# Two attention units to a turn, and three PSUM users on other banks, in a hybrid decoder layer

## The chip, the cores and the metric

The kernel runs on one core of a Trainium2 chip. The metric is the time of one execution in device microseconds (us), as the median of several runs. One further execution is taken by the hardware profiler; its page and its trace are what is read here. The engines are TensorE (PE in the rows; PEld is its weight load), VectorE (DVE), ScalarE (ACT), GpSimd (POOL) and SyncE (SP), which issues nearly all DMAs.

## What is computed

One decoder layer on x of 1024 x 2048 in float32: an RMS norm, one input projection to 6656 columns, two groups of attention heads side by side, a gated RMS norm of each, one output projection, and a second RMS norm added to x.

```python
def reference(x, w_in, w_out, norm_pre, norm_post, gn_sb, gn_sw, sinks, rel_bias):
    h = x
    for l in range(DEPTH):                                   # DEPTH = 1
        u = rmsnorm(h, norm_pre[l])
        proj = jnp.einsum('bsd,de->bse', u, w_in[l])
        q_sb, k_sb, v_sb, z_sb, q_sw, k_sw, v_sw, z_sw = jnp.split(proj, SPLIT_POINTS, axis=-1)
        o_sb = stick_breaking_attention(q_sb, k_sb, v_sb)    # 16 heads of 64
        o_sw = sliding_window_gqa(q_sw, k_sw, v_sw, sinks[l], rel_bias)  # 16 heads, 4 of K and V, window 128
        o_sb = rmsnorm(o_sb, gn_sb[l]) * jax.nn.silu(z_sb)
        o_sw = rmsnorm(o_sw, gn_sw[l]) * jax.nn.silu(z_sw)
        y = jnp.einsum('bse,ed->bsd', jnp.concatenate([o_sb, o_sw], axis=-1), w_out[l])
        h = h + rmsnorm(y, norm_post[l])
    return h
# stick-breaking: A[t,s] = beta_ts * prod_{s<j<t}(1 - beta_tj), beta = sigmoid(q.k / 8), s < t
# sliding window: softmax over q.k / 8 + bias, with one sink logit a head
```

## The kernel before

**Tiles and stages.** The input projection is done in 52 blocks of 128 columns. Each operand is split into a high and a low part, so a block is 16 x 2 x 3 matmuls of 128x512 (p_qsw, p_ksb and so on in the rows; three "first" blocks are f0a to f2b, done together while x arrives). Queries and keys go to DRAM and come back where attention wants them. The last stage, the output projection (rows y), is not touched.

**Units.** Attention is cut into 224 units: 64 of sliding-window heads (sw, in groups g = 0 to 3 of 16) and 160 of stick-breaking heads (sb, pairs 0 to 7 of 20 units; in a pair two heads, in a head four groups of 256 rows with 4, 3, 2 and 1 units). A unit has three stages on TensorE:

- s1: four score matmuls into a "pz" bank (z). Then ScalarE and VectorE make the weights: for sb two sigmoids, two scans and a product (tiles m and b; a unit on the diagonal is also masked on GpSimd), for sw a biased softmax (tile L, with an exponential that waits for the row maximum nm).
- s2: three or four transposes of the weights into a "pw" bank (wt; two in a group's last sw unit); ScalarE and VectorE split them into wh and wl.
- s3: four output matmuls (o; two in a group's last sw unit) into the "po" bank. After a sw unit, and after the last unit of a sb row group, ScalarE copies the bank out (finish_o, line 513, tile ot, two buffers), and the copy goes to DRAM.

**PSUM.** Eight banks: "pp" three (projections), "pz" two, "pw" two (also the transposes vt of V), "po" one.

**What sets the order.** TensorE's matmuls keep the order in which the program writes them. After every three projection matmuls `step()` calls `advance()`, which decides by `pe_time`, a running estimate of TensorE's time, whether attention gets a turn. A unit has a period (PER_SB 4.7, PER_SW 3.8), least distances between its stages (lag 6.2 or 7.0 from s1 to s2, lag2 4.5 or 5.0 from s2 to s3), and a depth: at most 3 units between s1 and s2. Before, a turn finishes all outputs that are due, the transposes of one unit, and starts one unit. At a V block's end `drain()` forces what is left of the group or pair. On the other engines a scheduler sets the order; copies out of PSUM have raised priority there.

Of the kernel before, what the change touches and what calls it, by code (L numbers as in the profile page):

```python
# [57 lines left out]
def layer(ctx, tc, xT, x, w_first, w_blk, w_out, g_pre, g_post, g_sb, g_sw, sinks, rel, onehot, penalty, out):  # L58
# [20 lines left out]
    def ptile(tag, name, bufs, shape=None):  # L79
        return pp.tile(shape or [P, HALF], F32, tag=tag, name=name, bufs=bufs)  # L80

    def pproj(name):
        return ptile("pp", name, 3)

    def pz(name, shape=None):
        return ptile("pz", name, 2, shape)

    def pw(name, shape=None):
        return ptile("pw", name, 2, shape)

    def po(name, shape=None):
        return ptile("po", name, 1, shape)
# [24 lines left out]
    def mm(ps, a, b, start, stop):  # L117
        n = 1
        for d in b.shape[1:]:
            n *= d  # L120
        pe_time[0] += n / 2400.0 * (4 if n < 256 or b.dtype == F32 else 1)
        tc.keep_in_program_order(nc.tensor.matmul(ps, a, b, start=start, stop=stop))  # L122
# [20 lines left out]
    waiting, todo = [], []  # L143
    stage1, stage2 = [], []
    last_start = [-100.0]
# [6 lines left out]
    def advance(force=False):  # L152
        now = pe_time[0]
        while waiting and (force or waiting[0][0] <= now):
            todo.extend(waiting.pop(0)[1])
            prep()
        if later and (force or later[0][0] <= now):
            later.pop(0)[1]()
            return True
        if force or not todo:  # L160
            return finish_stage2(force, now) or finish_stage1(force, now) or (bool(todo) and start(now))
        if len(stage1) - stage1_due(now) < todo[0]["depth"] and last_start[0] + todo[0]["period"] <= now:
            while finish_stage2(False, now):
                pass
            finish_stage1(False, now)
            return start(now)
        return False

    def start(now):
        if len(stage1) >= todo[0]["depth"]:  # L170
            return False
        u = todo.pop(0)
        if not u["ready"]:
            u["prep"]()
        last_start[0] = max(last_start[0] + u["period"], now - u["period"])
        u["s1"]()
        stage1.append((pe_time[0], u))
        prep()
        return True

    def stage1_due(now):
        return 1 if stage1 and len(stage2) < 3 and stage1[0][0] + stage1[0][1]["lag"] <= now else 0

    def finish_stage2(force, now):
        if stage2 and (force or stage2[0][0] + stage2[0][1]["lag2"] <= now):
            u = stage2.pop(0)[1]
            u["s3"]()
            left[u["key"]] -= 1
            return True
        return False  # L190

    def finish_stage1(force, now):
        if stage1 and len(stage2) < 3 and (force or stage1_due(now)):
            u = stage1.pop(0)[1]
            u["s2"]()
            stage2.append((pe_time[0], u))
            return True
        return False

    def prep():  # L200
        for u in todo[:AHEAD]:
            if not u["ready"]:
                u["ready"] = True
                u["prep"]()
# [66 lines left out]
    def step():  # L271
        advance()
        background()

    def drain(key):
        n = left.get(key, 0)
        while left.get(key, 0):
            assert advance(True)
        if n and DBG:
            print("DRAIN", key, n, f"{pe_time[0]:.0f}")  # L280
# [4 lines left out]

    xh, xl, xraw = [], [], []
    acc = stg.tile([P, S], F32, tag="acc", name="acc_x", bufs=1)
    ps0 = [[pproj("f0a"), pproj("f0b")], [pproj("f1a"), pz("f1b")], [pz("f2a"), pw("f2b")]]

    oh = at.tile([32, RW], F32, tag="beta", name="oh", bufs=3)  # L290
    pen = at.tile([P, RW], F32, tag="m", name="pen", bufs=3)
# [44 lines left out]
        nc.vector.tensor_scalar_mul(nsink, nsink, -1.0)  # L336

    def bias_table():
        pr = po("bias_ps")
        rel8 = at.tile([32, 16, 8], F32, tag="wl", name="rel8", bufs=3)  # L340
        nc.vector.tensor_copy(rel8, relt.unsqueeze(2).to_broadcast([32, 16, 8]))
        mm(pr[:, :RW], rel8, oh, start=True, stop=True)
        rt = at.tile([P, RW], F32, tag="m", name="rt", bufs=3)
        nc.vector.tensor_add(rt, pr[:, :RW], pen)
        nc.scalar.dma_start(biasd.rearrange("h (a r) n -> (h a) r n", a=8), rt.unsqueeze(1).to_broadcast([P, 16, RW]))

    def rstd_half(h):
        cols = slice(h * HALF, (h + 1) * HALF)
        ps = (pw, po)[h](f"ssq{h}")
        mm(ps, ones, acc[:, cols], start=True, stop=True)  # L350
        nc.scalar.activation(rstd[:, cols], ps, AF.Sqrt, bias=eps, scale=1.0 / D)
        nc.vector.reciprocal(rstd[:, cols], rstd[:, cols])
# [7 lines left out]
    for k in range(KT):  # L360
        if k + WAHEAD < KT:
            first.append(split_first(k + WAHEAD))
        if k + XAHEAD < KT:
            load_x(k + XAHEAD)
        if k == 5:
            load_small()
        if k == 10:
            bias_table()
        if k == KT - 3:
            rstd_half(0)  # L370
            rstd_half(1)
        wh, wl = first.pop(0)
        parts = [(b, h) for h in range(2) for b in range(len(FIRST))]
        for b, h in sorted(parts) if k == KT - 1 else parts:
            for i, (wt, xt) in enumerate(((wh, xh[k]), (wh, xl[k]), (wl, xh[k]))):
                mm(ps0[b][h], wt[:, b, :], xt[:, h * HALF:(h + 1) * HALF],
                   start=(k == 0 and i == 0), stop=(k == KT - 1 and i == 2))
        for i in (k,) if k < 8 else range(2 * k - 8, 2 * k - 6) if k < 12 else ():
            square_x(i)
# [92 lines left out]
    def proj(b, name, nxt=None, mid=None):  # L472
        def get(b, name, kg):
            return split_w(f"{name}_{kg}", w_blk[b, :, 4 * kg:4 * kg + 4, :])

        if not splits:
            splits.append(get(b, name, 0))
        ps = [pproj(f"p_{name}_{h}") for h in range(2)]
        for kg in range(4):
            wh, wl = splits.pop(0)  # L480
            if kg == 2 and mid is not None:
                mid()
            if kg < 3:
                splits.append(get(b, name, kg + 1))
            elif nxt is not None:
                splits.append(get(*nxt, 0))
            for h in range(2):
                for j in range(4):
                    k = 4 * kg + j
                    for i, (wt, xt) in enumerate(((wh, xh[k]), (wh, xl[k]), (wl, xh[k]))):  # L490
                        mm(ps[h], wt[:, j, :], xt[:, h * HALF:(h + 1) * HALF],
                           start=(k == 0 and i == 0), stop=(k == KT - 1 and i == 2))
                    step()
        return ps
# [349 lines left out]
    for n, (b, name, done) in enumerate(work):  # L844
# [3 lines left out]
        ps = proj(b, name, nxt, mids.get(name))  # L848
# [16 lines left out]
    def bank(name):  # L865
        tg = PT2[next(slots) % 8]
        return ptile(tg, name, PB[tg])
# [64 lines left out]
    for i in range(LAST + 1):  # L932
        nxt, src = [], []
        for dc in range(2):
            k0 = (2 * i + dc) * 8
            if i == LAST and dc == 1:
                split_wo(k0 + 8)
                for tb in range(4):
                    for h in range(1 + (tb == 3)):
                        part = slice(h * 256, (h + 1) * 256) if tb == 3 else whole  # L940
                        ps = bank(f"y{i}_{dc}_{tb}_{h}")[:, :part.stop - part.start]
# [8 lines left out]
            for e in range(8):  # L950
# [24 lines left out]
                if i == LAST and dc == 0:  # L975
                    tb, h = divmod(e, 2)
# [59 lines left out]
```

## Time and profile before

| | |
|---|---|
| median of 3 runs | 1795.58 us (1795.38 to 1796.92) |
| the profiled execution | 1792.82 us |
| its span, first to last instruction | 1791.0 us |
| granted TensorE clock, mean | 0.998 |
| TensorE busy, 112 to 480 us (sw attention) | 365.33 of 368 us |
| TensorE busy, 480 to 1430 us (sb attention) | 947.25 of 950 us |
| VectorE busy in the same two | 245.11, 677.64 us |
| ScalarE busy in the same two | 168.99, 407.95 us |

In a timeline row the first number is the start in us from the span's beginning, the second the duration in us, then engine, line, operation, out<-in, shape and count; in brackets stands how long the engine sat idle before it and what ended that. Matmuls overlap, and their ends are modelled, so what one costs is read from start to start.

### The profile page before, as it was taken

To read this page: it belongs to the slowest core of one execution; us is meant where nothing else is said; L and a number is where in the kernel's file an instruction comes from. 1 tells how busy PE (TensorE), PEld (TensorE's weight loads), DVE (VectorE), ACT (ScalarE), POOL (GpSimd) and SP (SyncE) were. 2 spreads that over 40 slices of the span, in tenths; PEclk is the share of its full clock that TensorE was granted. 3 is DMA by queue.
4 is the path that set the end of the run, shared out by engine and by line. 5 is a ranking of instruction groups with operands and counts; after the bars stand their busy time and mean duration, and the time that the engine had idled before them with its cause. 6 is when DMAs were issued, how large, how long until landed. Compare 5 with 4: busy or idle time off the path is not lost.

```text
span 1791.0 us, 27350 instructions
## 1 busy us (share of the span) xinstructions
PE 1769.0 (99%) x9046; PEld 1498.0 (84%) x9046; DVE 1230.8 (69%) x1984; ACT 783.2 (44%) x1696; POOL 498.5 (28%) x648
## 2 busy tenths in 40 slices
PE   8999999999999999999999999999999999999998
PEld 7788888888888888888888888888888887888886
DVE  7558842678467678586675777767868756845896
ACT  7345531455334444344443444434434434444442
POOL 0012121211213324323232333232313224503633
PEclk9999999999999999999999999999999999999999
DMA  7647675576746666556556564554445386634484
GB/s 232 195 149 217 201 228 159 161 204 195 226 131 190 172 177 183 167 170 203 157 162 191 155 186 131 154 165 141 149 109 139 93 257 204 208 101 141 135 283 157
DMA packets 203884, 312.48 MB, mean 174 GB/s; under 512 B 24640, under 2 KB 84192, under 8 KB 203616
## 3 DMA queue, kind: packets, MB, share of 16 engines
q1 hardware_dynamic: 201680, 307.60, 57.6%
q10 hardware_dynamic: 2064, 3.15, 0.5%
q8 instruction: 72, 1.18, 0.3%
q14 instruction: 68, 0.56, 0.1%
HBM read 219.42 MB, written 91.23 MB: 173 GB/s over the span
## 4 chain that ended last, share of the span: by engine, by line
PE 91%; DVE 4%; DMA 2%; ACT 1%; issue 1%; SPq 0%; DVEq 0%; POOL 0%; ACTq 0%; POOLq 0%
PE y L928 16%; PE p_zsw L122 10%; PE p_zsb L122 10%; PE p_vsb L122 9%; PE p_ksb L122 9%; PE p_qsw L122 8%; PE p_qsb L122 8%; PE o_sb L122 4%; PE z_sb L122 4%; PE wt_sb L126 3%; PE p_vsw L122 1%; PE z_sw L122 1%; PE o_sw L122 1%; PE wt_sw L126 1%; DVE wl_sw L661 1%; PE f0a L122 1%
## 5 line engine op out<-in xcount | busy, mean ns | idle before, releaser
L582 DVE TENSOR_TENSOR wl_sb<-wt_sb,wh_sb 128x512 fp32r<-128x512 f32 (+1 forms) x160 | 100.8, 633 | 96.6 <-ACT wh_sb L581 96.4
L566 DVE TENSOR_TENSOR b_sb<-b_sb,m_sb 128x512 f32<-128x512 f32 x160 | 129.5, 809 | 41.2 <-POOL b_sb L556 17.7
L581 ACT CAST wh_sb<-wt_sb 128x512 fp32r<-128x512 f32 (+1 forms) x160 | 87.0, 544 | 135.5 <-PE wt_sb L126 133.0
L563 DVE TENSOR_TENSOR_SCAN m_sb<-m_sb,m_sb,zero 128x257 f32<-128x257 f32 x192 | 142.4, 780 | 2.4 <-ACT m_sb L550 2.1
L928 PE MATMUL y<-wohi,x 128*128 128x512 f32 x448 | 140.7, 390 | 0.4 <-ACT wohi L792 0.4
L928 PE MATMUL y<-wohl,x 128*128 128x512 f32 x576 | 132.5, 389 | 0.0
L928 PEld LDWEIGHTS y<-wohl,x 128*128 128x128 f32 x576 | 108.1, 188 | 22.4
L560 DVE TENSOR_TENSOR_SCAN m_sb<-m_sb,mask 128x256 f32<-128x256 f32 x128 | 119.1, 967 | 6.4 <-ACT m_sb L550 6.3
L643 ACT ACTIVATE L_sw<-L_sw,nm_sw 128x256 f32<-128x256 f32 (+1 forms) x128 | 62.8, 491 | 94.9 <-DVE nm_sw L638 93.5
L122 PE MATMUL p_vsb<-xh,whi_vsb 128*128 128x512 f32 x256 | 101.9, 398 | 0.0
L122 PE MATMUL p_ksb<-xh,wlo_ksb 128*128 128x512 f32 x256 | 100.7, 393 | 0.0
L122 PE MATMUL p_qsb<-xh,whi_qsb 128*128 128x512 f32 x256 | 100.6, 393 | 0.0
L122 PE MATMUL p_vsb<-xh,wlo_vsb 128*128 128x512 f32 x256 | 100.6, 393 | 0.0
L122 PE MATMUL p_qsb<-xh,wlo_qsb 128*128 128x512 f32 x256 | 100.6, 393 | 0.0
L122 PE MATMUL p_zsw<-xh,wlo_zsw 128*128 128x512 f32 x256 | 100.6, 393 | 0.0
L122 PE MATMUL p_vsb<-xl,whi_vsb 128*128 128x512 f32 x256 | 100.5, 392 | 0.0
L122 PE MATMUL p_ksb<-xl,whi_ksb 128*128 128x512 f32 x256 | 100.4, 392 | 0.0
L122 PE MATMUL p_qsb<-xl,whi_qsb 128*128 128x512 f32 x256 | 100.4, 392 | 0.0
L122 PE MATMUL p_zsw<-xl,whi_zsw 128*128 128x512 f32 x256 | 100.4, 392 | 0.0
L122 PE MATMUL p_zsb<-xh,wlo_zsb 128*128 128x512 f32 x256 | 100.4, 392 | 0.0
L122 PE MATMUL p_zsb<-xl,whi_zsb 128*128 128x512 f32 x256 | 100.2, 391 | 0.0
L122 PE MATMUL p_zsb<-xh,whi_zsb 128*128 128x512 f32 x256 | 100.0, 391 | 0.0
(243 smaller groups left out, 4971.3 us busy)
## 6 DMA issues: line engine op xcount, KB each, us to landing
row_sw<-in_w_out SPq DMA_DIRECT2D x80, 256.0 KB, 4.4
bg<-in_w_out SPq DMA_DIRECT2D x80, 256.0 KB, 4.6
woraw<-wsum SPq DMA_DIRECT2D x80, 256.0 KB, 3.5
kh<-kd SPq DMA_DIRECT2D x160, 64.0 KB, 3.1
kl<-kd SPq DMA_DIRECT2D x160, 64.0 KB, 2.6
wsum<-row_sw SPq DMA_DIRECT2D x40, 256.0 KB, 3.0
wsum<-bg SPq DMA_DIRECT2D x40, 256.0 KB, 3.4
q_sw<-qd SPq DMA_DIRECT2D x64, 128.0 KB, 3.5
```

Source lines behind the costliest of these rows:

```text
L122: tc.keep_in_program_order(nc.tensor.matmul(ps, a, b, start=start, stop=stop))
L126: tc.keep_in_program_order(nc.tensor.transpose(ps, a, ident))
L560: nc.vector.tensor_tensor_scan(m[:, tb, 1:257], m[:, tb, 1:257], mask[:, P - P * tb:P - P * tb + 256], m[:, tb, 0:1], ALU.mult, ALU.max)
L563: nc.vector.tensor_tensor_scan(m[:, tb, :], m[:, tb, :], zero.to_broadcast([P, 257]), prev[:, tb, 256:257], ALU.mult, ALU.max)
L566: nc.vector.tensor_mul(beta, beta, m[:, :, 0:256])
L581: nc.scalar.copy(wh[:, :k], pt[:, :k])
L582: nc.vector.tensor_sub(wl[:, :k], pt[:, :k], wh[:, :k].bitcast(F32))
L643: nc.scalar.activation(L[:, hh, :n], L[:, hh, :n], AF.Exp, bias=nm[:, hh:hh + 1], accum_out=sm[:, hh:hh + 1])
L661: nc.vector.tensor_sub(wl[:, :nj], pt[:, :nj], wh[:, :nj].bitcast(F32))
L928: nc.tensor.matmul(ps, xt[:, a, tcols], w[b][:, cols], start=first and n == 0, stop=last and n == 2)
```

## The change

A turn comes once in two periods. It finishes one output, transposes up to two units, finishes all other outputs that are due, and starts two units (one, where the depth of 3 allows no more; then it tries again at the next step). The look-ahead `stage1_due` is gone. Three PSUM users move: half f2b of the first blocks from "pw" to "po", the bias table from "po" to "pw", and both sums of squares to "pw" (before one in "pw", one in "po").

```diff
         if force or not todo:
             return finish_stage2(force, now) or finish_stage1(force, now) or (bool(todo) and start(now))
-        if len(stage1) - stage1_due(now) < todo[0]["depth"] and last_start[0] + todo[0]["period"] <= now:
+        if last_start[0] + 2 * todo[0]["period"] <= now:
+            finish_stage2(False, now)
+            turned = finish_stage1(False, now) and finish_stage1(False, now)
             while finish_stage2(False, now):
                 pass
-            finish_stage1(False, now)
-            return start(now)
+            return start(now) and (not todo or start(now)) or turned
         return False
...
-    def stage1_due(now):
-        return 1 if stage1 and len(stage2) < 3 and stage1[0][0] + stage1[0][1]["lag"] <= now else 0
...
-        if stage1 and len(stage2) < 3 and (force or stage1_due(now)):
+        if stage1 and len(stage2) < 3 and (force or stage1[0][0] + stage1[0][1]["lag"] <= now):
...
-    ps0 = [[pproj("f0a"), pproj("f0b")], [pproj("f1a"), pz("f1b")], [pz("f2a"), pw("f2b")]]
+    ps0 = [[pproj("f0a"), pproj("f0b")], [pproj("f1a"), pz("f1b")], [pz("f2a"), po("f2b")]]
...
-        pr = po("bias_ps")
+        pr = pw("bias_ps")
...
-        ps = (pw, po)[h](f"ssq{h}")
+        ps = pw(f"ssq{h}")
```

Lines behind the edit stand two higher in the changed kernel (the copy of line 513 is 511 there).

TensorE, sliding-window group 0, around the output of unit 5 of the first head pair (o_sw0_5_0; the numbers at a name's end only count tiles). Before:

```order
L122 MATMUL p_qsw3_0_1298<-xh11_523,wlo_qsw3_2_1453 128x512
L122 MATMUL o_sw0_5_0_1577<-wh_sw0_5_0_1480,v_vsw0_0_832 128x256
L122 MATMUL o_sw0_5_0_1577<-wl_sw0_5_0_1481,v_vsw0_0_832 128x256
L122 MATMUL o_sw0_5_0_1577<-wh_sw0_5_0_1480,v_vsw0_0_832 128x256
L122 MATMUL o_sw0_5_0_1577<-wl_sw0_5_0_1481,v_vsw0_0_832 128x256
L126 MATMUL wt_sw0_7_0_1585<-ident_190,L_sw0_7_0_1431 128x128 x2
L122 MATMUL z_sw0_2_1_1592<-kh_1065,q_sw0_2_1_1446 128x256
```

One output, one unit's transposes, one unit's scores, and the projection before and behind. The same place on TensorE after:

```order
L122 MATMUL o_sw0_4_0_1607<-wl_sw0_4_0_1454,v_vsw0_0_832 128x256
L126 MATMUL wt_sw0_7_0_1615<-ident_190,L_sw0_7_0_1470 128x128 x2
L122 MATMUL o_sw0_5_0_1622<-wh_sw0_5_0_1513,v_vsw0_0_832 128x256
L122 MATMUL o_sw0_5_0_1622<-wl_sw0_5_0_1514,v_vsw0_0_832 128x256
L122 MATMUL o_sw0_5_0_1622<-wh_sw0_5_0_1513,v_vsw0_0_832 128x256
L122 MATMUL o_sw0_5_0_1622<-wl_sw0_5_0_1514,v_vsw0_0_832 128x256
L122 MATMUL o_sw0_6_0_1630<-wh_sw0_6_0_1522,v_vsw0_0_832 128x256
L122 MATMUL o_sw0_6_0_1630<-wl_sw0_6_0_1523,v_vsw0_0_832 128x256
L122 MATMUL o_sw0_6_0_1630<-wh_sw0_6_0_1522,v_vsw0_0_832 128x256
L122 MATMUL o_sw0_6_0_1630<-wl_sw0_6_0_1523,v_vsw0_0_832 128x256
L122 MATMUL z_sw0_2_1_1638<-kh_1065,q_sw0_2_1_1485 128x256
```

The outputs of units 4, 5 and 6 have moved into one turn, with one unit's transposes between the first two and nothing between the others.

ScalarE at the same place. Before (L643 is the softmax's exponential, L645 that of the sink, L513 the copy of an output, L660 the split of the transposed weights):

```order
L643 ACTIVATE L_sw0_0_1_1489,sm_sw0_0_1_1496<-L_sw0_0_1_1489,nm_sw0_0_1_1491 128x256 x2
L645 ACTIVATE es_sw0_0_1_1494<-es_sw0_0_1_1494 128x2
L513 COPY ot_sw0_4_0_1524<-o_sw0_4_0_1519 128x256
L133 CAST whi_qsw3_3_1561<-wraw_qsw3_3_1559 128x512
L660 CAST wh_sw0_6_0_1532<-wt_sw0_6_0_1527 128x512
L643 ACTIVATE L_sw0_1_1_1541,sm_sw0_1_1_1548<-L_sw0_1_1_1541,nm_sw0_1_1_1543 128x256
L513 COPY ot_sw0_5_0_1582<-o_sw0_5_0_1577 128x256
```

Exponentials stand between the copies of units 4 and 5. After:

```order
L643 ACTIVATE es_sw0_1_1_1556<-es_sw0_1_1_1556 128x2
L391 CAST hi_qsw3_0_1668<-u_qsw3_0_1666 128x512
L511 COPY ot_sw0_4_0_1612<-o_sw0_4_0_1607 128x256
L658 CAST wh_sw0_7_0_1618<-wt_sw0_7_0_1615 128x256
L511 COPY ot_sw0_5_0_1627<-o_sw0_5_0_1622 128x256
L511 COPY ot_sw0_6_0_1635<-o_sw0_6_0_1630 128x256
```

The three copies have moved together, behind all exponentials of the turns before.

TensorE, stick-breaking pair 3, where its row group 3 of the first head begins (o_sb3_0_3). Before:

```order
L122 MATMUL p_zsw6_0_9838<-xh10_487,wlo_zsw6_2_9933 128x512
L122 MATMUL o_sb3_0_3_10012<-wh_sb3_0_3_3_9910,v_vsb3_0_9227 128x256
L122 MATMUL o_sb3_0_3_10012<-wl_sb3_0_3_3_9911,v_vsb3_0_9227 128x256
L122 MATMUL o_sb3_0_3_10012<-wh_sb3_0_3_3_9910,v_vsb3_0_9227 128x256
L122 MATMUL o_sb3_0_3_10012<-wl_sb3_0_3_3_9911,v_vsb3_0_9227 128x256
L126 MATMUL wt_sb3_1_0_1_10020<-ident_190,b_sb3_1_0_1_9878 128x128 x4
L122 MATMUL z_sb3_1_1_1_10029<-kh_1065,q_sb3_1_0_9647 128x256
```

There a projection stands ahead of the output. After:

```order
L122 MATMUL o_sb3_0_2_9864<-wl_sb3_0_2_3_9851,v_vsb3_0_9223 128x256
L126 MATMUL wt_sb3_1_0_0_9948<-ident_190,b_sb3_1_0_0_9876 128x128 x3
L126 MATMUL wt_sb3_1_0_1_9958<-ident_190,b_sb3_1_0_1_9894 128x128 x4
L122 MATMUL o_sb3_0_3_9967<-wh_sb3_0_3_3_9858,v_vsb3_0_9223 128x256
L122 MATMUL o_sb3_0_3_9967<-wl_sb3_0_3_3_9859,v_vsb3_0_9223 128x256
L122 MATMUL o_sb3_0_3_9967<-wh_sb3_0_3_3_9858,v_vsb3_0_9223 128x256
L122 MATMUL o_sb3_0_3_9967<-wl_sb3_0_3_3_9859,v_vsb3_0_9223 128x256
L122 MATMUL z_sb3_1_0_2_9975<-kh_1065,q_sb3_1_0_9664 128x256
```

The last output of row group 2 and the first of group 3 have moved into one turn, with two units' transposes between them.

## The prediction

> **What bounds the kernel now.** I read the page's busy time and chain first, then TensorE's own waits, then its timeline.
>
> ```profile
> span 1791.0 us, 27350 instructions
> PE 1769.0 (99%) x9046; PEld 1498.0 (84%) x9046; DVE 1230.8 (69%) x1984; ACT 783.2 (44%) x1696; POOL 498.5 (28%) x648
> PE 91%; DVE 4%; DMA 2%; ACT 1%; issue 1%; SPq 0%; DVEq 0%; POOL 0%; ACTq 0%; POOLq 0%
> ```
>
> TensorE is busy for the whole span and is 91% of the chain that ended last. So a change of the order counts by two things: what it does to the spacing of TensorE's matmuls, and what it makes TensorE wait for. Nearly nothing makes it wait today (columns: total us, times, longest):
>
> ```profile
> PE f0a L122 <- ACT whi_f L327: 5.8, 1, 5.8
> PE wt_sb L126 <- DVE wl_sb L582: 1.9, 1, 1.9
> PE o_sw L122 <- ACT ot_sw L513: 1.9, 5, 0.7
> PE vt_vsw L126 <- DVE v_vsw L415: 1.9, 1, 1.9
> PE o_sb L122 <- ACT ot_sb L513: 0.8, 1, 0.8
> ```
>
> The first row is the wait for the first weights. The third and fifth are the ones to keep in mind: an output matmul that waits until ScalarE has copied the previous output out of the one "po" bank.
>
> A turn of one stick-breaking unit, from TensorE's timeline (start, duration; ends are modelled, so I count from start to start):
>
> ```profile
> 902.84 0.28 PE L122 MATMUL o_sb<-wl_sb,v_vsb 128*128 128x256 f32 x1
> 902.96 0.49 PE L126 MATMUL wt_sb<-ident,b_sb 128*128 128x128 f32 x3
> 903.21 0.36 PE L122 MATMUL z_sb<-kh,q_sb 128*128 128x256 f32 x1
> 903.41 0.28 PE L122 MATMUL z_sb<-kl,q_sb 128*128 128x256 f32 x1
> 903.52 0.28 PE L122 MATMUL z_sb<-kh,q_sb 128*128 128x256 f32 x1
> ...
> 903.76 0.39 PE L122 MATMUL p_ksb<-xh,whi_ksb 128*128 128x512 f32 x1
> ...
> 905.84 0.39 PE L122 MATMUL p_zsw<-xh,whi_zsw 128*128 128x512 f32 x1
> ...
> 907.88 0.28 PE L122 MATMUL o_sb<-wh_sb,v_vsb 128*128 128x256 f32 x1
> ```
>
> Three things are seen. A 256-wide matmul takes 0.12 us and a transpose 0.25/3 = 0.083. The first matmul behind transposes takes 0.20 (903.21 to 903.41) where the next takes 0.11 to 0.12: leaving the transposes costs 0.08. And the first nine projection matmuls after the turn take 2.08 us (903.76 to 905.84), the next nine 2.04: coming back from attention costs 0.04.
>
> **What the change gains.** Counted in TensorE's order, runs of transposes fall from 244 to 152, since two units' transposes now stand together: 92 x 0.08 = 7.4 us. Returns to the projections fall from 326 to 198. Of these 128, 90 had nine or more projection matmuls behind them, so that the whole 0.04 was paid: 3.6 us; the short ones I count at nothing.
>
> The swap of banks frees a "pw" bank at the start. The second transpose of the first V block waits there:
>
> ```profile
> 88.61 0.42 DVE L415 TENSOR_TENSOR v_vsw<-vt_vsw,v_vsw 128x256 fp32r<-128x256 f32 x1
> 89.18 0.63 PE L126 MATMUL vt_vsw<-ident,u_vsw 128*128 128x128 f32 x4 [1.86 <-DVE v_vsw L415]
> ...
> 89.84 0.69 DVE L385 TENSOR_TENSOR u_qsw<-f2b,rstd 128x512 f32<-128x512 f32 x1 [0.81 <-PE vt_vsw L126]
> ```
>
> It takes the bank of the first, while f2b holds the other; with f2b in "po", the program's second transpose no longer waits for the first's readers. That is 1.9 us. The other moves of the swap cost nothing: f2b is read out of "po" at 90 us, and outputs want it much later (one of the first stands at 130.29 below); bias and sums of squares have two "pw" banks that nothing else uses then. The 2.7 us of output waits above I count as gone too, because what replaces them is priced anew below. Together: 7.4 + 3.6 + 1.9 + 2.7 = 15.6 us.
>
> **What the change costs: outputs back to back.** Two units' outputs now stand in one turn, and all outputs share one "po" bank. So the second must wait until ScalarE has copied the first out. What such a hand-over takes is in the trace:
>
> ```profile
> 130.29 0.28 PE L122 MATMUL o_sw<-wl_sw,v_vsw 128*128 128x256 f32 x1
> 130.61 0.37 ACT L513 COPY ot_sw<-o_sw 128x256 f32<-128x256 f32 x1 [1.83 <-PE o_sw L122]
> ...
> 242.56 0.28 PE L122 MATMUL o_sw<-wl_sw,v_vsw 128*128 128x256 f32 x1
> 242.93 0.37 ACT L513 COPY ot_sw<-o_sw 128x256 f32<-128x256 f32 x1 [1.27 <-PE o_sw L122]
> 243.38 0.36 PE L122 MATMUL o_sw<-wh_sw,v_vsw 128*128 128x256 f32 x1
> 243.57 0.28 PE L122 MATMUL o_sw<-wl_sw,v_vsw 128*128 128x256 f32 x1
> ```
>
> In both, ScalarE sat idle and started as soon as it could: 0.32 and 0.37 us after the last output matmul's start. The copy takes 0.37, the next output starts 0.08 after its end. In total 0.82 in the second case; with the first's 0.32 it is 0.77. I take 0.76, near the quicker of the two. The first matmul after a wait takes 0.19 (243.38 to 243.57): 0.07 more.
>
> How often, by the order of the changed program:
> - 26 outputs directly behind another unit's (18 sliding-window, 8 at the end of a stick-breaking pair): 0.76 − 0.12 + 0.07 = 0.71 each, 18.5 us.
> - 18 sliding-window outputs with only one unit's transposes between: 16 with four (0.12 + 4 x 0.083 = 0.45 pass anyway, 0.31 is waited), 2 with two (0.47 waited); the price of leaving the transposes is in the 152 already: 5.9 us.
> - 16 stick-breaking outputs that begin a new row group, with seven transposes between (0.70): 0.06 each, 1.0 us.
>
> Sum 25.4 us, against nothing of the kind where one unit a turn is handled. In stick-breaking the other outputs of a pair add to the same sum and need no copy, which is why it suffers less.
>
> ScalarE isn't always free when the copy is due. A late case, and the waits of the outputs' weight loads:
>
> ```profile
> 183.28 0.19 ACT L643 ACTIVATION_READ_ACCUMULATOR L_sw<-L_sw,nm_sw 128x1 f32 x1
> 183.37 0.35 ACT L513 COPY ot_sw<-o_sw 128x256 f32<-128x256 f32 x1
> 183.77 0.39 PE L122 MATMUL o_sw<-wh_sw,v_vsw 128*128 128x256 f32 x1 [0.38 <-ACT ot_sw L513]
> ...
> PEld o_sw L122 <- ACT ot_sw L513: 5.0, 9, 1.1
> ```
>
> Here the copy stood behind an exponential. Nine times before, a copy came so late that even an output a whole turn later waited, 5.0/9 = 0.56 us each, 1.1 at worst. In the changed order the exponentials ahead of a copy are about a turn and a half old, so it should be better than that: I take half, 0.28, at the 18 turns of the second kind, and 0.2 at the 16 of the third: 8 us. The ends are 0, and 1.1 at the 18 with 0.5 at the 16: 28.
>
> **What the change costs: the pair's chain.** Before, a stick-breaking unit's scores are turned into weights over two other turns; now a pair must be done by the next. In the order 33 projection matmuls lie between, 33 x 2.04/9 = 7.5 us, with the turn's own output (0.48) and the first unit's transposes (0.33), 8.3 us. The work on VectorE (count | busy, mean ns | idle):
>
> ```profile
> L563 DVE TENSOR_TENSOR_SCAN m_sb<-m_sb,m_sb,zero 128x257 f32<-128x257 f32 x192 | 142.4, 780 | 2.4 <-ACT m_sb L550 2.1
> L566 DVE TENSOR_TENSOR b_sb<-b_sb,m_sb 128x512 f32<-128x512 f32 x160 | 129.5, 809 | 41.2 <-POOL b_sb L556 17.7 <-POOL m_sb L554 10.1 <-ACT whi_zsb L133 0.5
> L560 DVE TENSOR_TENSOR_SCAN m_sb<-m_sb,mask 128x256 f32<-128x256 f32 x126 | 117.4, 968 | 5.3 <-ACT m_sb L550 5.2
> L135 DVE TENSOR_TENSOR wlo_vsb<-wraw_vsb,whi_vsb 128x512 fp32r<-128x512 f32 x28 | 23.1, 826 | 0.9 <-ACT whi_vsb L133 0.7
> L550 ACT ACTIVATE m_sb<-z_sb 128x512 f32<-128x512 f32 x160 | 96.7, 604 | 6.7 <-PE z_sb L122 4.1 <-ACT wh_sb L581 0.4
> ...
> L563 DVE TENSOR_TENSOR_SCAN m_sb<-m_sb,m_sb,zero x192: 720/740/2921, 509.8 to 1412.3; 128x257 f32<-128x257 f32 x192
> ```
>
> A sigmoid (0.6), four scans (0.78 to 0.97), two products (0.81) and one weight split (0.83) make 6.2 to 6.9 us. It fits, with 1.4 to 2.1 us to spare; but one slow scan (2.92 at worst, 0.74 the median) or a masked product that waits for GpSimd (17.7 us in all) uses that up. There are 80 such pairs. If one in eight is late by 0.5 us, it is 5 us; the ends are 0 and 15.
>
> **The sum.** −15.6 + 25.4 + 8 + 5 = +22.8. The profiled execution took 1792.82 us, 1.8 around its span; the median of the runs is 1795.58, 2.8 above it. On the median: 1818.
>
> [...]
>
> **Rivals.**
> - Faster: the hand-over hides. With one term, its length H, gains and costs balance where 26(H − 0.05) + 16(H − 0.45) + 2(H − 0.29) = 15.6, at H = 0.56. If outputs are handed over more quickly than that, and nothing is late, the change wins; with H at 0.4 the direct ones cost 9 us and the rest nothing, and the time is 1789. Against it: the copy alone is 0.37, the quickest start behind the matmul 0.32, 0.69 in all. Chance 0.06; within 0.2% (3.6 us, about what a measurement of this kernel can tell from no change) 0.04.
> - Slower still: the pairs come late. If copies and chains stand at their upper ends (28 and 15), it is −15.6 + 25.4 + 43 = +53, 1848. For it: the copies of three outputs run close together, with two staging buffers. Against: ScalarE is 44% busy. Chance 0.13 for more than 1836.
> - The clock falls. This trace has the slow state at the start alone: 0.42 us a matmul from the first at 5.8 us on, 0.23 from 9.76 on. If each of 44 waits brought that back, half of these four microseconds 44 times would make some 88 us, 1906.
>
> ```profile
> 8.50 0.63 PE L122 MATMUL f2a<-xh,whi_f 128*128 128x512 f32 x1
> 8.92 0.63 PE L122 MATMUL f2a<-xl,whi_f 128*128 128x512 f32 x1
> ...
> 9.76 0.39 PE L122 MATMUL f0b<-xh,whi_f 128*128 128x512 f32 x1
> 9.99 0.39 PE L122 MATMUL f0b<-xl,whi_f 128*128 128x512 f32 x1
> ...
> 837.00:843.00 6.00, 4.07 (x22) 3.15 (x21) 2.92 (x5) 0.85 (x2) 2.41 (x6) 1.00 0.84 214
> ```
>
> The last row (granted clock third from the end) is the stretch with a wait of 1.9 us: 1.00. Chance 0.02. [...]
>
> **Chances and range.** The forecast, slower by 7 to 40 us, has 0.75; the rest is above, so slower 0.90, same 0.04, faster 0.06. With no copy or chain late the sum is +9.8, 1805; the shortest hand-over (0.74: 0.32, 0.37, and 0.05 as at 183.77) takes 1 more off. Leaving out about one in ten on either side, the range is 1802 to 1838.
>
> **What would show it.** In the changed profile, TensorE should wait some 25 to 35 us for ot_sw and ot_sb (2.7 before), most of it under o_sw between 110 and 480 us; vt_vsw's 1.9 should be gone; the first matmuls behind transposes should fall in number with the same 0.20. Waits of wt_sb for b_sb should be a few microseconds. I am wrong if o_sw's waits are under 10 us (the hand-over is quicker than its rows), or if wt_sb's waits exceed o_sw's (the chain is the bound).

## The result, and the profile after

The changed kernel takes 1829.26 us (median of 4 runs, 1827.15 to 1829.93) against 1795.48 us (4 runs, 1794.99 to 1796.92) before: a ratio of 1.0186, 95% interval 1.0173 to 1.0200, or 33.8 us more. 1818 us was forecast, with a range of 1802 to 1838: slower as said, by 11 us more than said.

The profiled execution of the changed kernel took 1829.93 us. The page's span, its busy times, and the chain that ended last:

```profile
span 1828.2 us, 27265 instructions
PE 1783.4 (98%) x9046; PEld 1506.5 (82%) x9046; DVE 1248.4 (68%) x1984; ACT 784.5 (43%) x1696; POOL 507.0 (28%) x648
PE 34%; DVE 2%; DMA 1%; issue 1%; ACT 1%; POOL 0%; SPq 0%; DVEq 0%; ACTq 0%; POOLq 0%
```

The shares of the chain add up to 39% here, so the page follows it back over a part of the span only, and nothing below rests on its 34%. No engine has more to do than before. The span grew by 37.2 us; every engine has as many instructions as before. TensorE's matmuls are no more than they were, so its 14 us of further busy time can only be slower ones and the way their ends are modelled. What is new are TensorE's waits (us in total, times, longest):

```profile
PE o_sw L122 <- ACT ot_sw L511: 12.8, 22, 2.4
PE o_sb L122 <- ACT ot_sb L511: 8.9, 8, 4.9
PE wt_sb L126 <- DVE b_sb L564: 3.2, 4, 1.6
PE p_vsb L122 <- DVE wlo_vsb L135: 1.6, 1, 1.6
```

The two rows of outputs stood at 1.9 and 0.8 us before. Now they are 21.7, and that is not all: a row counts a wait only under the engine that ended it by the profile, and some direct hand-overs stand there under other names (one is shown below under a DMA). So I counted start to start in TensorE's order. A turn with three outputs, which are those of the front part's second place, then ScalarE's copies:

```profile
153.76 0.28 PE L122 MATMUL o_sw<-wl_sw,v_vsw 128*128 128x256 f32 x1
153.88 0.38 PE L126 MATMUL wt_sw<-ident,L_sw 128*128 128x128 f32 x2
154.50 0.39 PE L122 MATMUL o_sw<-wh_sw,v_vsw 128*128 128x256 f32 x1 [0.24 <-ACT ot_sw L511]
154.73 0.28 PE L122 MATMUL o_sw<-wl_sw,v_vsw 128*128 128x256 f32 x1
154.84 0.29 PE L122 MATMUL o_sw<-wh_sw,v_vsw 128*128 128x256 f32 x1
154.97 0.28 PE L122 MATMUL o_sw<-wl_sw,v_vsw 128*128 128x256 f32 x1
155.71 0.38 PE L122 MATMUL o_sw<-wh_sw,v_vsw 128*128 128x256 f32 x1 [0.46 <-ACT ot_sw L511]
155.93 0.28 PE L122 MATMUL o_sw<-wl_sw,v_vsw 128*128 128x256 f32 x1
...
154.08 0.37 ACT L511 COPY ot_sw<-o_sw 128x256 f32<-128x256 f32 x1 [0.43 <-PE o_sw L122]
155.28 0.37 ACT L511 COPY ot_sw<-o_sw 128x256 f32<-128x256 f32 x1 [0.55 <-PE o_sw L122]
```

The first wait has two transposes ahead of it: 153.88 to 154.50. The second has nothing: 154.97, copy at 155.28 (0.31 later, 0.37 long), next output at 155.71. That is 0.74 from last matmul to first, where the prediction took 0.76, and 0.22 instead of 0.12 to the matmul behind. All 18 direct sliding-window hand-overs are 0.74 or 0.75; thirteen of the sixteen with four transposes pass in 0.62 or 0.63 from the first transpose; six of the eight at a stick-breaking pair's end take 0.83 or 0.84.

Where the 37.2 us of the span went, counted between starts of TensorE's matmuls (the excess over a plain spacing of 0.227 for a projection, 0.12 for scores and outputs, 0.085 for a transpose, from the first score to the first y row; before, then after):

| | before | after |
|---|---|---|
| outputs directly behind outputs (26) | 0 | 21.5 |
| outputs behind a turn's transposes | 0 | 11.5 |
| output matmuls themselves, the one behind a wait above all | 0.8 | 3.3 |
| outputs behind projections | 3.7 | 0.6 |
| at transposes, and at the first matmul behind them | 21.8 | 20.8 |
| transposes that wait for VectorE | 3.3 | 4.3 |
| projections: spacing | 11.4 | 11.9 |
| projections that wait for weights or others | 0.7 | 3.2 |
| scores | -1.2 | -0.2 |

The first two rows are 33 us; the table's differences add up to 36.4. By the timeline's stages, 21.0 us were lost between the first sliding-window and the first stick-breaking score, 15.9 from there to the first y row, 0.3 elsewhere.

### The profile page after: what moved, and what is told of

Read it like the earlier page. It is cut to its first block, busy times and chain, and to the rows that moved or that the text cites. A ratio compares the mean times of both kernels' runs of the same rounds, so it can differ in the third digit from the quotient of the medians.

```text
span 1828.2 us, 27265 instructions
## 1 busy us (share of the span) xinstructions
PE 1783.4 (98%) x9046; PEld 1506.5 (82%) x9046; DVE 1248.4 (68%) x1984; ACT 784.5 (43%) x1696; POOL 507.0 (28%) x648
## 5 line engine op out<-in xcount | busy, mean ns | idle before, releaser
L580 DVE TENSOR_TENSOR wl_sb<-wt_sb,wh_sb 128x512 fp32r<-128x512 f32 (+1 forms) x160 | 96.4, 633 | 113.3 <-ACT wh_sb L579 113.0
L579 ACT CAST wh_sb<-wt_sb 128x512 fp32r<-128x512 f32 (+1 forms) x160 | 81.7, 546 | 146.2 <-PE wt_sb L126 145.7
L558 DVE TENSOR_TENSOR_SCAN m_sb<-m_sb,mask 128x256 f32<-128x256 f32 x128 | 135.2, 1091 | 8.8 <-ACT m_sb L548 8.6
L564 DVE TENSOR_TENSOR b_sb<-b_sb,m_sb 128x512 f32<-128x512 f32 x160 | 123.6, 773 | 17.5 <-POOL b_sb L554 9.5
L548 ACT ACTIVATE m_sb<-z_sb 128x512 f32<-128x512 f32 x160 | 97.0, 606 | 20.8 <-PE z_sb L122 14.3
L122 PE MATMUL p_ksb<-xh,whi_ksb 128*128 128x512 f32 x256 | 100.6, 393 | 0.0
L926 PEld LDWEIGHTS y<-wohi,x 128*128 128x128 f32 x448 | 84.1, 188 | 19.3 <-ACT wohi L790 1.7
L122 PE MATMUL p_zsw<-xh,whi_zsw 128*128 128x512 f32 x256 | 99.9, 390 | 0.0
```

What stands on the lines that cost most here:

```text
L548: nc.scalar.activation(m[:, :, 1:257], z, AF.Sigmoid, scale=-SCALE)
L558: nc.vector.tensor_tensor_scan(m[:, tb, 1:257], m[:, tb, 1:257], mask[:, P - P * tb:P - P * tb + 256], m[:, tb, 0:1], ALU.mult, ALU.max)
L564: nc.vector.tensor_mul(beta, beta, m[:, :, 0:256])
L579: nc.scalar.copy(wh[:, :k], pt[:, :k])
L580: nc.vector.tensor_sub(wl[:, :k], pt[:, :k], wh[:, :k].bitcast(F32))
L926: nc.tensor.matmul(ps, xt[:, a, tcols], w[b][:, cols], start=first and n == 0, stop=last and n == 2)
```

## The experiments

The theory to be tested: outputs that follow each other closely wait for their one bank, and that is the loss. Its rivals: handling units in pairs makes VectorE's and ScalarE's chains late; the bank moves cost something. Ratios are to the kernel before on the same chip, with 95% intervals; a thousandth is 1.8 us.

**The bank moves alone**, in the kernel before.

```diff
-    ps0 = [[pproj("f0a"), pproj("f0b")], [pproj("f1a"), pz("f1b")], [pz("f2a"), pw("f2b")]]
+    ps0 = [[pproj("f0a"), pproj("f0b")], [pproj("f1a"), pz("f1b")], [pz("f2a"), po("f2b")]]
-        pr = po("bias_ps")
+        pr = pw("bias_ps")
-        ps = (pw, po)[h](f"ssq{h}")
+        ps = pw(f"ssq{h}")
```

> The three bank moves alone, with the turns of before. Theory (the loss comes from outputs that wait for their one bank): the moves cost nothing; at most the 1.9 us of the V transposes' wait at the start go, and the changed kernel's trace gave most of that back in slow first matmuls. 1793.5 to 1795.5 us. Rival (the moves themselves cost, because the first blocks or the sums now wait for banks): 1798 us or more.

Measured: 1793.29 us against 1797.42, ratio 0.9982 (0.9971 to 0.9994). The moves cost nothing and gain a little. The same kernel once more, beside another one below:

> The bank moves alone once more, beside the kernel above on the same chip. Theory: ratio to before 0.998 as the first time; above 0.9995 the first was chance.

Measured: 1793.47 against 1795.59, ratio 0.9989 (0.9975 to 1.0003): again below 1, though here the interval reaches it. In the traces the first score stands at 107.63 and 108.35 us (before 109.43), and no wait of vt_vsw is left. That is the predicted wait at the start, less what the first matmuls took from it; where the rest of the gain lies is not shown.

**The new turns alone**, as the changed kernel with the moves undone.

```diff
-    ps0 = [[pproj("f0a"), pproj("f0b")], [pproj("f1a"), pz("f1b")], [pz("f2a"), po("f2b")]]
+    ps0 = [[pproj("f0a"), pproj("f0b")], [pproj("f1a"), pz("f1b")], [pz("f2a"), pw("f2b")]]
-        pr = pw("bias_ps")
+        pr = po("bias_ps")
-        ps = pw(f"ssq{h}")
+        ps = (pw, po)[h](f"ssq{h}")
```

> The new turns with the banks of before. The bank moves alone had gained some 3 us (ratio 0.998), of which the trace shows 1.8 before the first score. Theory (both parts add up): 1829 + 2 to 3 = 1831 to 1832 us, and the V transposes' wait at the start back. Rival (in the changed kernel the moves gained nothing, because slow first matmuls gave it back): 1829.

Measured: 1834.48 us, ratio 1.0209 (1.0187 to 1.0231), against the whole change's 1.0186: 4 us above it, with vt_vsw's wait of 1.9 us back in the trace. The two intervals overlap, so the size is rough; that the turns make the whole loss is clear.

**Outputs apart, units still in pairs.** The second output of a turn moves between the scores of the two new units.

```diff
-            while finish_stage2(False, now):
-                pass
-            return start(now) and (not todo or start(now)) or turned
+            started = start(now)
+            finish_stage2(False, now)
+            return started and (not todo or start(now)) or turned
```

> Two units a turn as in the changed kernel, but a turn now finishes one output, transposes two units, starts one, finishes a second output, and starts the other; a third output waits for the next turn. By its order, outputs that stand directly behind another bank user fall from 26 to 7, and those with one unit's transposes between from 18 to 0; four score matmuls (0.48 us) stand between instead. Theory (the hand-over of the one output bank costs it): of 33 us of waits behind outputs some 28 go, with them about 5 us of slow matmuls behind the long ones and 2 us of first matmuls behind a wait: 1794 us (1790 to 1800). Rival (handling units in pairs costs it, because the pair's chain on VectorE and ScalarE comes late): the pairs are as before this edit, so 1820 us or more, with waits of transposes for VectorE.

Measured: 1799.94 us, ratio 1.0016 (1.0005 to 1.0027). Of 0.0186 only 0.0016 is left, though units still come in pairs. TensorE's waits:

```profile
PE o_sb L122 <- ACT ot_sb L511: 4.9, 8, 0.9
PE p_vsb L122 <- DVE wlo_vsb L135: 2.9, 3, 2.5
PE o_sw L122 <- ACT ot_sw L511: 2.2, 4, 1.0
...
PE wt_sb L126 <- DVE b_sb L564: 0.7, 2, 0.5
```

By the count above, waits ahead of outputs fall from 33.6 to 9.5 us, the projections' spacing from 11.9 to 6.7. The theory stands and the pairs' chain falls as the main cause: its row, b_sb, is 0.7 us. The 4.9 of o_sb are mostly the seven outputs that still follow another directly at a pair's end.

**Those too.** When no unit is left to start, an output comes due earlier.

```diff
-        if stage2 and (force or stage2[0][0] + stage2[0][1]["lag2"] <= now):
+        if stage2 and (force or stage2[0][0] + stage2[0][1]["lag2"] - (0 if todo else 2.0) <= now):
```

> The kernel with outputs apart, and at a group's or pair's end, when no unit is left to start, outputs come due 2.0 us of the program's own clock earlier, so that a projection stands between the last two. By its order no output stands directly behind another one any more. Theory: the 5.3 us that the 7 of these still waited go; 1793 us, ratio to before 0.999 (0.997 to 1.000). Rival (the last outputs then wait for their own weights from VectorE instead): no change, ratio 1.0015.

Measured: 1797.20 against 1797.17, ratio 0.9998 (0.9986 to 1.0010): 3 us less than without, and no change against before. The direct waits (5.3) are gone from the trace, but one output still waits 3 us, at 1081.7 us, now behind a projection; what that is comes below.

**At most two outputs a turn.** Only sliding-window's direct hand-overs go, 16 of 18.

```diff
-            while finish_stage2(False, now):
-                pass
+            finish_stage2(False, now)
```

> The changed kernel, but a turn finishes two outputs at most; a third waits for the next turn. By the order, sliding-window outputs directly behind another fall from 18 to 2, all other hand-overs stay. Theory (each direct hand-over costs 0.62 of wait and some 0.07 at the matmul behind it): 16 x 0.69 = 11 us less than the changed kernel, 1818 us on the scale of the prediction. Rival (the waits come from ScalarE being late behind the exponentials, so the turn's one remaining output waits as long): 1826 or more.

Measured: 1814.81 us, ratio 1.0101 (1.0083 to 1.0118), so 15 us less than the change, where 11 was expected. Direct waits fall from 21.5 to 11.5 us as reckoned; the rest is the first matmuls behind them and the slow projections (11.9 to 8.6) that followed long waits.

**The copy twice.** One suspected cost is doubled.

```diff
             nc.scalar.copy(ot, ops[:, :256])
+            nc.scalar.copy(ot, ops[:, :256])
```

> The changed kernel with every output's copy out of PSUM done twice, one behind the other, into the same buffer. Theory (a hand-over is the copy plus fixed parts, and TensorE waits for all of it): 0.37 to 0.40 more at 44 outputs (17 us), and 0.3 at the 16 with seven transposes between (5): 22 us over the changed kernel, 1851. Rival (the loss lies in the pair's chain, and ScalarE has idle time): 1829 to 1833.

Measured: 1860.99 us, ratio 1.0358 (1.0339 to 1.0376): 31 us over the change, more than expected. The place of 154.97 above, TensorE and then ScalarE:

```profile
155.55 0.28 PE L122 MATMUL o_sw<-wl_sw,v_vsw 128*128 128x256 f32 x1
156.70 0.38 PE L122 MATMUL o_sw<-wh_sw,v_vsw 128*128 128x256 f32 x1 [0.87 <-ACT ot_sw L512]
...
155.87 0.37 ACT L511 COPY ot_sw<-o_sw 128x256 f32<-128x256 f32 x1 [0.83 <-PE o_sw L122]
156.28 0.37 ACT L512 COPY ot_sw<-o_sw 128x256 f32<-128x256 f32 x1
```

1.15 where it was 0.74: TensorE pays the second copy in full, 0.41. At all 18 direct sliding-window hand-overs it is 1.14 or 1.15. The 9 us beyond the expected 22 lie in places that the expectation left out: outputs behind projections wait again (10 of them, 5.2 us), and most that begin a row group behind seven transposes take longer than the 1.12 of the quickest (first transpose to output), up to 1.48, as ScalarE comes late.

**Two banks for outputs.** One is taken from the projections.

```diff
-        return ptile("pp", name, 3)
+        return ptile("pp", name, 2)
-        return ptile("po", name, 1, shape)
+        return ptile("po", name, 2, shape)
-    ps0 = [[pproj("f0a"), pproj("f0b")], [pproj("f1a"), pz("f1b")], [pz("f2a"), po("f2b")]]
+    ps0 = [[pproj("f0a"), pproj("f0b")], [po("f1a"), pz("f1b")], [pz("f2a"), po("f2b")]]
...
-    PT2 = ("pz", "pz", "pw", "pw", "po", "pp", "pp", "pp")
-    PB = {"pp": 3, "pz": 2, "pw": 2, "po": 1}
+    PT2 = ("pz", "pz", "pw", "pw", "po", "po", "pp", "pp")
+    PB = {"pp": 2, "pz": 2, "pw": 2, "po": 2}
```

The last four lines name the same banks to the output projection.

> The changed kernel with two banks for the outputs instead of one, and two for the projections instead of three. The order is the changed kernel's, word for word. Theory (one output bank): an output no longer waits for the copy of the one just before it; all 44 short waits and the long ones go, 33 + 5 + 2 us: 1789 us, and up to 10 us more if the projections miss their third bank (52 blocks x 0.2): 1789 to 1799. Rival (pairs come late): 1822 us or more. Second rival (the projections need their third bank): waits of p rows for the reads of VectorE or ScalarE, over 15 us, and 1805 or more.

Measured: 1813.59 us, ratio 1.0099 (1.0080 to 1.0118): better than the change by 16 us, but in the time of the second rival (1805 or more). TensorE's waits (ten rows of p for u add up to 13 us):

```profile
PE o_sw L122 <- ACT ot_sw L511: 6.9, 7, 2.0
...
PE p_zsw L122 <- DVE u_ksb L383: 3.0, 3, 1.6
...
PE p_vsb L122 <- DVE u_zsw L383: 1.9, 4, 0.6
PE p_zsw L122 <- DVE u_zsw L383: 1.7, 1, 1.7
```

By the count from start to start, waits ahead of outputs fall from 33.6 to 8.7 us: one bank was the cause of most of them. But the projections now wait for VectorE to read out their bank, and that gives 13 us back. The third bank of the projections is worth about half of what a second one for outputs brings (13 against 24.9 us here); the order is the cheaper cure.

**Transposes apart too.** As the kernel with outputs apart, with each unit's transposes by themselves, so that their runs go back from 152 to 244.

```diff
-            turned = finish_stage1(False, now) and finish_stage1(False, now)
+            turned = finish_stage1(False, now)
             started = start(now)
             finish_stage2(False, now)
+            finish_stage1(False, now)
             return started and (not todo or start(now)) or turned
```

> As the kernel with outputs apart, but the transposes apart too: a turn finishes an output, transposes one unit, starts one, finishes a second output, transposes the second unit, starts the other. Runs of transposes go back from 152 to 244, returns to the projections stay few (202). The first is what the prediction priced at 92 x 0.08 = 7.4 us. If that price is right: 7.4 us above the kernel with outputs apart (ratio to before 1.006). If a transpose costs 0.11 wherever it stands, and the 0.08 behind it is only its early start stamp: within 2 us of that kernel (ratio 1.001), with the sum of the excess at and behind transposes at some 21 us as in all kernels so far.

Measured: 1803.74 us, ratio 1.0034 (1.0022 to 1.0046), 3 us above the kernel with outputs apart: neither theory's number. The count settles it: the excess at and behind transposes is 21.35 us here and 21.34 there, with 242 and 150 runs. The difference in time is elsewhere, in waits ahead of outputs (12.6 against 9.5) and slow projections (8.9 against 6.7).

**One kind of unit in pairs.** The other goes by the turns of before. For stick-breaking in pairs (with "sw" in place of "sb" for the other kernel):

```diff
+        if todo[0]["key"][:2] != "sb":
+            due = 1 if stage1 and len(stage2) < 3 and stage1[0][0] + stage1[0][1]["lag"] <= now else 0
+            if len(stage1) - due < todo[0]["depth"] and last_start[0] + todo[0]["period"] <= now:
+                while finish_stage2(False, now):
+                    pass
+                finish_stage1(False, now)
+                return start(now)
+            return False
         if last_start[0] + 2 * todo[0]["period"] <= now:
```

> Two units a turn for stick-breaking alone; sliding-window units go by the turns of before. Theory (18 + 18 of the 60 hand-overs with a wait are sliding-window's): from the first sliding-window score to the first stick-breaking score the changed kernel had lost 21.0 us, behind it 15.9; so 1829 - 21 = 1808 us (1805 to 1811). Rival (the stick-breaking pair's chain costs most, and sliding window only its outputs): 1815 us or more.

Measured for stick-breaking alone: 1808.78 us, ratio 1.0069 (1.0053 to 1.0085), 1807.9 on the scale of 1795.5, as expected.

> Two units a turn for sliding-window units alone (with the bank moves); stick-breaking goes by the turns of before. The counterpart had stick-breaking paired alone, at ratio 1.0069. Theory (the two stages add up): 1.0186 - 1.0069 + 0.9982 = 1.0099, 1813 us (1809 to 1817). Rival (the stages are coupled through late units that one hands to the other): off by more than 5 us.

Measured for sliding window alone: 1821.74 us, ratio 1.0136 (1.0114 to 1.0158), 1819.9 on that scale: 7 us above the expectation. The sum of the two stages misses, as the rival had it, but not by the late units that it named. Sliding window's own stage is 24.0 us longer than with the bank moves alone, against 21.0 in the change; the rest is in stick-breaking, whose code and order of turns are those of before. Its waits have a row of 6.5 us, 4.2 of it in one place. GpSimd, VectorE and TensorE there:

```profile
PE wt_sb L126 <- DVE wl_sb L588: 6.5, 2, 4.2
...
861.39 1.29 POOL L252 TENSOR_TENSOR row_sw<-row_sw 128x512 f32<-128x512 f32 x1 [3.81 <-DMA row_sw<-in_w_out]
864.28 1.26 POOL L252 TENSOR_TENSOR bg<-bg 128x512 f32<-128x512 f32 x1 [1.59 <-DMA bg<-in_w_out]
865.49 0.62 POOL L562 TENSOR_SCALAR_AFFINE_SELECT b_sb<-b_sb 128x512 f32<-128x512 f32 x1
866.15 0.69 DVE L572 TENSOR_TENSOR b_sb<-b_sb,m_sb 128x512 f32<-128x512 f32 x1 [6.28 <-POOL b_sb L562]
867.36 1.15 DVE L588 TENSOR_TENSOR wl_sb<-wt_sb,wh_sb 128x384 fp32r<-128x384 f32 x2
867.96 0.90 PE L126 MATMUL wt_sb<-ident,b_sb 128*128 128x128 f32 x3 [4.21 <-DVE wl_sb L588]
```

Read it upward: TensorE wants a "pw" bank, whose reader wl_sb stands on VectorE behind b_sb; b_sb waits 6.28 us for a mask on GpSimd; the mask stands in GpSimd's queue behind two background sums of output weights (row_sw, bg), and each of them waited for its DMA (3.81 and 1.59 us). The granted clock is 0.50 for 6.83 us from 866.39 on, around this wait, and for 3.41 us behind the other wait of the row, from 630.87 on; the projections behind the two waits start 0.43 apart (869.09 to 869.52, 632.40 to 632.83) where 0.23 is usual (862.20 to 862.42), and that makes further microseconds of this stage. The kernel before has the same wait, 1.9 us, at 841 us; the bank moves alone had two of it in one trace (2.4 us in all) and none in the other. So what a turn meets of the background transfers is worth up to some 4 us, and can be part of any total here; no run isolates it.

**Sliding window in pairs with outputs apart, stick-breaking as before.** The parts that looked best, put together: on the kernel with sliding window alone in pairs, the edit that sets outputs apart.

```diff
-            while finish_stage2(False, now):
-                pass
-            return start(now) and (not todo or start(now)) or turned
+            started = start(now)
+            finish_stage2(False, now)
+            return started and (not todo or start(now)) or turned
```

> The bank moves, sliding-window units two to a turn with their outputs apart, stick-breaking units by the turns of before. From the first sliding-window score to the first stick-breaking score, outputs apart took 395.1 us where the bank moves alone took 396.0. Theory: 1 us less than the bank moves alone, ratio to before 0.998 (0.9965 to 0.999). Rival (paired units bring slow matmuls or late copies in this stage): 0.999 or more.

Measured: 1795.34 us, ratio 0.9993 (0.9980 to 1.0006), beside 0.9989 for the bank moves alone on the same chip: no gain over them, as the rival had it, though the interval reaches the theory's 0.998. The best kernel here is the bank moves without the new turns: ahead of the kernel before by 0.1 and 0.2% in its two comparisons, of which one excludes no difference and one does not.

## Why the prediction was right, and where its sizes were off

**The sign and the mechanism** were right: the hand-over of the single bank. Predicted with a start-to-start time of 0.76, it is 0.74, and its pieces (0.31, 0.37, 0.06) are those that the two rows of the kernel before showed. Without its long cases, the hand-over's waits make 24 us and the matmuls behind them 2.5, against 25.4 predicted.

**Late copies**: predicted 8 (0 to 28), measured 9.1 above the ordinary hand-over. The size is right by luck: the 5.0 us in nine waits that it was taken from are those of weight loads, which overlap matmuls (in that trace PEld is busy for 84% of the span and PE for 99%), while the matmuls' own row was 1.9 us in five. And the way it comes is not as said: not a little at 34 turns, but nearly all in three places, 1.8, 2.4 and 4.3 us. The second on ScalarE, and the output on TensorE that waits for it:

```profile
197.14 0.51 ACT L641 ACTIVATE L_sw<-L_sw,nm_sw 128x256 f32<-128x256 f32 x1 [1.62 <-DVE nm_sw L636]
...
198.24 0.21 ACT L643 ACTIVATE es_sw<-es_sw 128x2 f32<-128x2 f32 x1
198.35 0.35 ACT L511 COPY ot_sw<-o_sw 128x256 f32<-128x256 f32 x1
...
198.75 0.38 PE L122 MATMUL o_sw<-wh_sw,v_vsw 128*128 128x256 f32 x1 [2.43 <-ACT ot_sw L511]
...
199.96 0.39 PE L122 MATMUL o_sw<-wh_sw,v_vsw 128*128 128x256 f32 x1 [0.46 <-DMA kd<-hi_ksw]
```

The copy was behind an exponential that itself waited for VectorE (nm). The argument that exponentials would be a turn and a half old, and so done, missed that they wait for VectorE in their turn. (The last row is a hand-over that the profile names a DMA.) The third place is longer and has another head, here on GpSimd and ScalarE, then TensorE:

```profile
1109.56 1.26 POOL L429 TENSOR_TENSOR or_zsb<-or_zsb 128x512 f32<-128x512 f32 x1 [10.22 <-DMA or_zsb<-od]
...
1110.85 0.63 ACT L447 ACTIVATE acc_sb<-or_zsb 128x512 f32<-128x512 f32 x1 [7.36 <-POOL m_sb L552]
1111.38 0.60 ACT L133 CAST whi_qsb<-wraw_qsb 128x512 fp32r<-128x512 f32 x1
1111.89 0.36 ACT L511 COPY ot_sb<-o_sb 128x256 f32<-128x256 f32 x1
...
1112.40 0.55 PE L122 MATMUL o_sb<-wh_sb,v_vsb 128*128 128x256 f32 x1 [4.86 <-ACT ot_sb L511]
...
1113.39 0.63 PE L122 MATMUL p_qsb<-xh,whi_qsb 128*128 128x512 f32 x1
1113.82 0.63 PE L122 MATMUL p_qsb<-xl,whi_qsb 128*128 128x512 f32 x1
```

The first sum of squares (acc_sb) of stick-breaking waits on ScalarE for GpSimd, GpSimd for attention outputs that come back from DRAM, and the copy stands behind. This place recurs: at 1137 us with the copy doubled (5.0), at 1115 in the new turns alone (5.7), and it is the 3 us that is left at 1081.7 with all outputs apart. The kernel before has acc_sb's wait too (2.9 us on ScalarE), but there no output needed its bank at that moment.

**Fewer runs of transposes**: predicted a gain of 7.4, measured about 1. This is the largest error. It read the 0.20 at the first matmul behind transposes as a price for leaving them. Eight in a row, after:

```profile
548.13 1.04 PE L126 MATMUL wt_sb<-ident,b_sb 128*128 128x128 f32 x8
548.92 0.36 PE L122 MATMUL o_sb<-wh_sb,v_vsb 128*128 128x256 f32 x1
549.12 0.28 PE L122 MATMUL o_sb<-wl_sb,v_vsb 128*128 128x256 f32 x1
```

From the first transpose to the second matmul it is 0.99 for eight, and 0.45 in the prediction's row for three: 0.54 for five more, 0.108 each. And 3 x 0.108 + 0.12 is 0.45: nothing is left for leaving. So by these two runs a transpose costs 0.108 among three as among eight; that the first matmul's start stamp is early is my reading of it. The kernels with 242 and 150 runs and the same 21.3 us agree.

**Fewer returns to the projections**: predicted 3.6, measured some 4.6 in the projections' spacing (11.4 to 6.8, once the slow matmuls below are taken out; the kernel with outputs apart, where few waits are left, has 6.7).

**The clock**: a rival with a chance of 0.02, "if each of 44 waits brought that back". The ordinary ones do not: behind 155.93 the matmuls are at normal pace (scores 0.12 apart from 156.29 on, projections 0.23 from 156.76 on). But behind three of the long ones (2.43, 1.83 and 4.86 us in the profile) it came back: the granted clock of this trace is 0.50 for 3.41 us from 200.36 on, as long from 432.47 on, and for 6.83 us from 1111.72 on. Behind 1112.40 the projections start 0.43 apart (1113.39 to 1113.82) instead of 0.23, for 12 matmuls; the three together cost 5.1 us in projections and about 1 in scores, and so gave back the gain of the returns. The mean clock of the stretch 112 to 480 us (third number from the end) fell to 0.99:

```profile
112.00:480.00 368.00, 354.84 (x1845) 298.57 (x1844) 241.71 (x615) 161.80 (x495) 65.50 (x50) 0.99 0.62 180
```

**The bank swap**: predicted 1.9, the traces show 1.1 and 1.8 with the moves alone, but in the profiled execution of the change only 0.3 (first score at 109.09): its first weights came 0.6 us later, and its first 14 matmuls ran slow (0.43 apart) instead of 9.

**The pair's chain**: predicted 5 (0 to 15). Transposes that wait for VectorE rose by 1 net (3.1 more behind transposes, 2.1 less behind projections), projections that wait for weights by 2.6, together under the 5. What the prediction named as its test holds: o_sw's waits are above 10 us, and wt_sb's are below them.

**Old waits of outputs**: predicted 2.7 gone, 3.1 are.

The sum: 22.8 was predicted for one execution against another, 37.2 is the difference of the two profiled spans. Of the 14.4 missed, 6.4 are the transposes, 6 the slow clock behind long waits, 1.6 the start, and the rest is made of pieces of 1 us. The medians differ by 33.8, since the two profiled executions stand 2.7 below and 0.7 above theirs.

## What to carry to other kernels

Where several producers share one PSUM bank, count how often two of them follow each other without enough other work between, and price each by matmul end, copy and restart; here 0.62 us at 26 places and half of it at 18 outweighed all that fewer switches of TensorE could bring. Writing other work between them (the scores) removed nearly all of it (ratio 1.0186 to 1.0016), where a second bank taken from another user gave much of it back (13 us). A price per switch is read from two run lengths, not from the stamp behind one.

## What the runs showed of the hardware

The granted clock fell behind some waits and not behind others. In the trace of the change TensorE was busy for 1.14, 1.62 and 0.00 us in the 3.41 us ahead of 200.36, 432.47 and 1111.72, and from there the clock was 0.50. In the kernel before it was busy for 1.56 us between 839.18 and 842.59, around the wait of 1.9 us at which the prediction saw the clock stay: 1.00 in that stretch and in the next 3.41 us. Here are two waits at the same place of p_vsb, each with a stretch that holds most of it or all, and the stretch behind: first with outputs apart (a wait of 2.53 us that ends at 598.50), then with those at a pair's end apart too (2.0 us, ending at 598.62). Behind the length stands TensorE's busy time; the granted clock is the third number from the end.

```profile
594.48:597.89 3.41, 1.50 (x7) 0.92 (x5) 3.41 (x4) 0.62 (x1) 2.19 (x2) 1.00 0.63 219
597.89:601.31 3.42, 2.81 (x20) 2.63 (x21) 1.81 (x4) 0.66 (x2) 0.39 (x3) 1.00 0.40 112
...
596.48:599.90 3.42, 1.40 (x8) 1.10 (x8) 3.29 (x5) 0.10 (x1) 0.32 (x1) 1.00 0.18 62
599.90:603.32 3.42, 3.42 (x19) 3.42 (x18) 1.16 (x2) 1.51 (x3) 0.46 (x3) 0.50 0.60 165
```

The longer wait left the clock at 1.00 in both of its stretches; behind the shorter one the next stretch is at 0.50. So the length of a wait does not tell by itself (2.53 us without a fall, 1.83 and 2.0 with one), and neither does TensorE's busy time in its stretch (1.62 us with a fall, 1.50 and 1.56 without). What decides it is not shown here.
